# A decoder step on one core: direct fp32 head sums, another start order, and later places for solver and group-norm results

## The chip, the cores and the metric

One core of one Trainium2 chip. The metric is device time in microseconds of one execution. Five engines work side by side, each with its own instruction stream: PE (TensorE, matmuls), DVE (VectorE), ACT (ScalarE), POOL (GpSimd), SP (SyncE, here only for issuing DMAs). ACT issues DMAs too, from its own queue.

## What is computed

One layer of a hybrid decoder: an RMSNorm, one input projection, an RWKV-7 branch with 8 heads of 64, a causal pooling branch, gates, an output projection and a final norm; 2048 prompt rows and 8 x 4 sample rows, all fp32. The part around the change is the RWKV recurrence, which the kernel computes in chunks of 64 steps:

```python
h = _rmsnorm(x, norm_w)
proj = jnp.einsum('btd,de->bte', h, w_in)
...
kk = heads(k * k_k)
kk = kk * lax.rsqrt(jnp.sum(kk * kk, axis=-1, keepdims=True) + L2_EPS)
...
def _wkv_step(S, inp):
    r, w, k, v, kk, a = inp
    sa = jnp.einsum('bhvk,bhk->bhv', S, -kk)
    S = S * w[:, :, None, :] + sa[..., None] * (kk * a)[:, :, None, :] + v[..., None] * k[:, :, None, :]
    y = jnp.einsum('bhvk,bhk->bhv', S, r)
    return S, y
...
mu = jnp.mean(y, axis=-1, keepdims=True)
var = jnp.mean(jnp.square(y - mu), axis=-1, keepdims=True)
y = ((y - mu) * lax.rsqrt(var + GN_EPS)).reshape(B, T, D_RWKV) * gn_w + gn_b
bonus = jnp.sum(r * k * r_k, axis=-1, keepdims=True) * v
o_rwkv = (y + bonus.reshape(B, T, D_RWKV)) * jax.nn.silu(g_rwkv)
```

Two sums over the 64 channels of a head occur per unit of work: the sum of kk squared, called `sq`, and the bonus sum, called `bo`.

## The kernel before

The 2048 prompt rows are worked in 4 groups g of 512, the channels of the RWKV branch in 4 pairs of heads j; a **unit** (g, j) is one pair in one group, 16 in all. The projection has 25 column tiles of 128. Tile 12 (the low-rank inputs, `pp_first` in group 0) comes first in a group; then each unit projects six tiles: r, k, pooling input, v and two gates. A tile is 8 steps over the contraction, each of three matmuls of 128x128 on 128x512 in F32R: the weight is split into a rounded high part `wh` and a remainder `wl`, the input into `xh` and `xl`, and the products wh·xh, wh·xl and wl·xh are added up (L345 to L347). In group 0 the weights are loaded raw (`wr`) and split by ACT and DVE (`w_split`), and the parts are stored to memory; later groups load the stored parts.

Everything else is threaded between these matmuls. `proj` yields after each of its eight steps; this is a **slot**, and a unit has 48 of them. In each slot `side()` (L449) takes one step of every lane: the solver (`solve`), the late generators (`late`), the products (`prod`), the fold and the chain. A generator places its work by the number of its bare `yield`s; these numbers (DH, DZ, DP, YQ and constants in the code) are the table that sets the order. In a lane only the first generator runs, the others wait behind it, so a later step in one unit's solver makes those behind it later too. Each engine runs its stream in order, and an instruction whose input is not there holds up all behind it.

A unit runs as follows. `shift` takes the k tile out of PSUM into `kps` (ACT L370, DVE L371 and L373). ACT squares it into `kk2` (L533). DVE makes `abd` (L536), `cs` (L540) and both halves of `bk` (L541, L545). `key_norms` computes the head sums: `head_sums` splits its input into `hi` (ACT L472, named h_sq, h_bo) and `lo` (DVE L474, l_sq, l_bo), and `head_sums_mm` multiplies both by a block matrix of ones `bonr` (L479, L480). `products` multiplies bk by abd into `pa` (PE L588), after three yields. `solve` writes the small triangular systems to memory, reads them back as L (L647 scales them), and POOL eliminates in 31 steps into X (L654, L656); POOL then masks F and rb (L666, L668), and after YQ = 16 slots PE transposes X (`xt`, L676). Fold and `pair_chain` (L774 `ch`, `z`, `f`) carry the state through the chunks; `pair_back` normalises each head's output Y on DVE (`group_norm`, with `rsqrt_newton`'s small steps at L55 to L57, last L801) and after five yields transposes it on PE (`try`, L811). An output projection follows at the end (L1160 to L1163).

At the start `first_x` loads the eight input tiles of group 0, makes their high and low parts and their squares, and POOL adds the squares up (`acc`, L263); `first_norm` turns the sum into row sums (`xsum`, L271) and the norm's factor, by which the finished tiles are scaled. The wait of a tile for its buffer follows from the tags: `bones` shares the tag `xn` with two of the first inputs, h_sq and h_bo share `kps` with k, and l_sq and l_bo share `rps` with r.

## Time and profile before

| What | Value |
|---|---|
| Median of 3 runs | 1274.54 us (1274.52 to 1277.41) |
| The profiled execution | 1273.72 us, its span 1272.0 us |
| Mean granted TensorE clock in it | 0.972 of full speed |
| PE busy | 1186.1 us, 93% |
| DVE busy | 830.7 us, 65% |
| ACT busy | 563.4 us, 44% |
| POOL busy | 500.9 us, 39% |
| Data moved | 200.18 MB, mean 157 GB/s |

The profiled execution is one run on the chip, recorded by the hardware profiler; its span is 1.7 us shorter than its time. The page gives each engine's busy time. The list of waits gives, for an engine, what ended each stretch of idle time: the instruction that waited, what released it, the total, the number of times and the longest. A timeline row has the start, the duration, the engine, the line, the output and the inputs, and in brackets the idle time ahead of it. Durations of PE rows overlap, since matmuls are pipelined: the time that one costs is the distance between starts. The table of windows gives busy times and the granted clock of a stretch, where 1.00 is 2.4 GHz and 0.50 is 1.2 GHz.

### The profile page before, as it was taken

What the parts mean: (1) busy time and instruction counts of PE and PEld (TensorE: products, weight loads), DVE (VectorE), ACT (ScalarE), POOL (GpSimd) and SP (SyncE); (2) the same over time, 40 slices, a digit from 0 to 9 for tenths busy, and PEclk for the clock granted to TensorE, in tenths of its full rate; (3) what the DMA queues carried; (4) which work ended last, traced back from release to release, by engine and by line L of the source; (5) the groups of instructions that cost most, each with busy time, mean ns of one, the idle gap of its engine ahead of it and who ended that gap; (6) DMA issues with size and microseconds to landing.
All of it is one profiled execution on the core that took longest, in us unless ns stands there. A gap on an engine that the chain in (4) does not pass through costs nothing. (4 is left out here: it accounts for less than half of the span.)

```text
span 1272.0 us, 21094 instructions
## 1 busy us (share of the span) xinstructions
PE 1186.1 (93%) x7229; PEld 977.9 (77%) x7229; DVE 830.7 (65%) x2028; ACT 563.4 (44%) x1363; POOL 500.9 (39%) x1138
## 2 busy tenths in 40 slices
PE   7996999889989999999899899989999999999997
PEld 4765777677878788788687789889889877887685
DVE  6845767857566756866576767564656577745764
ACT  4563645444445444546353546453535453321112
POOL 6054728172343754818064708270808370000000
PEclk7997999999999999999999999999999999999999
DMA  7774555454566554546374556444444444433431
GB/s 248 236 245 138 204 184 192 155 187 153 142 208 173 169 144 144 175 150 205 116 201 140 148 154 184 131 149 126 137 130 140 121 147 151 149 112 99 131 110 66
DMA packets 153372, 200.18 MB, mean 157 GB/s; under 512 B 82480, under 2 KB 99120, under 8 KB 153264
## 3 DMA queue, kind: packets, MB, share of 16 engines
q1 hardware_dynamic: 109632, 104.90, 26.9%
q10 hardware_dynamic: 43632, 93.93, 23.6%
q8 instruction: 57, 0.93, 0.3%
q14 instruction: 51, 0.42, 0.1%
HBM read 139.39 MB, written 46.80 MB: 146 GB/s over the span
## 5 line engine op out<-in xcount | busy, mean ns | idle before, releaser
L345 PE MATMUL pp<-xh,wh 128*128 128x512 f32 (+1 forms) x992 | 366.3, 370 | 8.8 <-ACT xh L204 5.3
L346 PE MATMUL pp<-xl,wh 128*128 128x512 f32 (+1 forms) x992 | 363.4, 366 | 1.3 <-DVE xl L205 1.2
L347 PE MATMUL pp<-xh,wl 128*128 128x512 f32 (+1 forms) x992 | 362.4, 366 | 0.5 <-DVE wl L325 0.5
L345 PEld LDWEIGHTS pp<-xh,wh 128*128 128x128 f32 x992 | 189.4, 191 | 34.5 <-ACT xh L204 6.3
L346 PEld LDWEIGHTS pp<-xl,wh 128*128 128x128 f32 x992 | 189.5, 191 | 24.9 <-DVE xl L205 2.4
L347 PEld LDWEIGHTS pp<-xh,wl 128*128 128x128 f32 x992 | 189.1, 191 | 24.1 <-DVE wl L325 1.8
L654 POOL TENSOR_TENSOR Xt<-X,L 128x60 f32<-128x60 f32 (+24 forms) x496 | 186.3, 376 | 38.9
L656 POOL TENSOR_TENSOR X<-X,Xt 128x60 f32<-128x60 f32 (+24 forms) x496 | 183.0, 369 | 38.9
L649 POOL TENSOR_TENSOR X<-dmask,a 128x256 f32<-128x256 bf16 x16 | 10.8, 675 | 288.8 <-DVE a L646 288.8
L647 POOL TENSOR_TENSOR L<-L,a 128x1024 f32<-128x1024 f32 x16 | 31.8, 1990 | 170.4 <-DMA L<-dA 170.4
L774 PEld LDWEIGHTS ch<-SV,F 128*128 128x128 f32 x512 | 74.5, 191 | 18.6 <-ACT Y L778 8.5
L774 PE MATMUL ch<-SV,F 128*128 128x64 f32 x512 | 79.5, 266 | 2.2 <-DVE F L744 0.9
L741 PE MATMUL f<-zbd,ka 128*128 128x256 f32 x256 | 68.2, 387 | 0.6 <-DVE zbd L736 0.3
L1160 PE MATMUL po_o<-woh,oh_o 128*128 128x512 f32 x160 | 66.8, 418 | 0.0
L776 DVE TENSOR_TENSOR SV<-ch,lc 64x128 f32<-64x128 f32 x112 | 33.0, 295 | 51.2 <-PE ch L774 46.6
L1163 PE MATMUL po_o<-woh,ol_o 128*128 128x512 f32 x160 | 65.1, 407 | 0.2 <-DVE ol_o L1151 0.2
L1161 PE MATMUL po_o<-wol,oh_o 128*128 128x512 f32 x160 | 65.1, 407 | 0.0
L588 PE MATMUL pa<-bk,abd 128*128 128x192 f32 x256 | 54.4, 358 | 10.2 <-DVE bk L545 6.3
L736 DVE COPY zbd<-z 64x256 f32<-64x256 f32 x64 | 27.1, 427 | 53.8 <-ACT zbd L735 52.7
L778 ACT ACTIVATE Y<-ch 64x128 f32<-64x128 f32 x128 | 34.2, 267 | 61.6 <-DVE SV L776 55.7
L744 DVE TENSOR_TENSOR F<-f,F 128x512 f32<-128x512 f32 x64 | 44.2, 690 | 25.8 <-PE f L741 22.4
L588 PEld LDWEIGHTS pa<-bk,abd 128*128 128x128 f32 x256 | 47.8, 211 | 15.4 <-issue 6.6
(447 smaller groups left out, 2330.1 us busy)
## 6 DMA issues: line engine op xcount, KB each, us to landing
wh<-wh ACTq DMA_DIRECT2D x75, 512.0 KB
wl<-wl ACTq DMA_DIRECT2D x75, 512.0 KB
wr<-in_w_in ACTq DMA_DIRECT2D x25, 512.0 KB
wh<-wh SPq DMA_DIRECT2D x25, 512.0 KB
wl<-wl SPq DMA_DIRECT2D x25, 512.0 KB
xr<-in_xT SPq DMA_DIRECT2D x32, 256.0 KB
L<-dA SPq DMA_DIRECT2D x64, 128.0 KB
oi<-o_d SPq DMA_DIRECT2D x16, 512.0 KB
```

What stands on the lines that cost most here:

```text
L345: PE.matmul(pp[:, :w], hi[:, kc, :], xh[:, c], start=(kc == 0), stop=False)
L346: PE.matmul(pp[:, :w], hi[:, kc, :], xl[:, c], start=False, stop=False)
L347: mark[0] = PE.matmul(pp[:, :w], lo[:, kc, :], xh[:, c], start=False, stop=(kc == KC - 1)).ins
L588: PE.matmul(pa[:, c, :], abd[:, 2 * b + c, :], bk[:, 2 * b + c, :], start=True, stop=True)
L654: GP.tensor_tensor(out=tm, in0=X[:, :n, i:i + 1].broadcast_to([P, n, w]), in1=L[:, i + 1:, i].unsqueeze(1).broadcast_to([P, n, w]), op=mult)
L656: done = GP.tensor_tensor(out=X[:, :n, i + 1:], in0=X[:, :n, i + 1:], in1=tm, op=add).ins
L741: PE.matmul(f[:, c].rearrange("p h t -> p (h t)"), u["ka"][:, 2 * b + c, :], zbd[b % 2][:, c].rearrange("p h t -> p (h t)"), start=True, s ...
L744: V.tensor_tensor(out=d, in0=f, in1=d, op=add)
L774: PE.matmul(ch[:, h, :], fm[cc // 4][:, cc % 4, h, :], sv[cc // 4][:, cc % 4, h, :], start=True, stop=True)
L1160: PE.matmul(pp[:m], hi[:, c, :m], wh, start=(c == 0), stop=False)
L1161: mark[0] = PE.matmul(pp[:m], hi[:, c, :m], wl, start=False, stop=(both and c == 7)).ins
L1163: mark[0] = PE.matmul(pp[:n], lo[:, c, :n], wh, start=False, stop=(c == 7)).ins
```

## The change

It has four parts.

- **Head sums.** `head_sums` multiplies the fp32 input by the block matrix in one fp32 matmul; the split on ACT, the remainder on DVE and the second matmul go. `sq` is placed 4 yields after its input, `bo` 4 after that (DH 6 to 4, and without the two extra). `prod` moves to the tag `rps`.
- **Start.** A small Tanh (`warm_act`) stands first on ACT, so the activation table is loaded there. `bones` moves from tag `xn` to `cs`. The first weight tile is loaded in four parts of 128x256 and split in four parts, each ahead of the two input tiles that it meets; all eight input loads are issued ahead of the second weight; weights 1 and 2 are loaded from SP's queue. All `xh` are made by ACT; the squares come later, from the sixth input tile on. `xsum` is placed one yield later, the broadcast of the factor one less behind it.
- **Solver.** In unit (0,0) alone xt comes 12 slots later (YQ + 12).
- **Places.** `products` waits five yields in place of three, `pair_back` nine in place of five.

```diff
@@ -82,11 +82,13 @@
         for _ in range(13):
             PE.matmul(wb, wu[:, 0:P], wu, start=True, stop=True)
 
+        A.activation(sb.tile([P, 4], F32, tag="rs", name="warm_act"), wu[:, 0:4], AF.Tanh)
+
     ident = cp.tile([P, P], F32, tag="ident", name="ident")
     make_identity(nc, ident)
     ones = cp.tile([P, P], F32, tag="ones", name="ones")
     GP.memset(ones, 1.0)
-    bones = sb.tile([P, P], F32, tag="xn", name="bones")
+    bones = sb.tile([P, P], F32, tag="cs", name="bones", bufs=1)
     GP.memset(bones, 0.0)
     for h in range(2):
         GP.memset(bones[64 * h:64 * h + 64, 64 * h:64 * h + 64], 1.0)
@@ -243,34 +245,40 @@
             raw.append(sb.tile([P, 512], F32, tag=("xr", "xn", "F", "sg")[kc % 4], name=f"xr_0_{kc}",
                                bufs=3 if kc % 4 == 2 else 2))
             nc.sync.dma_start(raw[kc], xT[kc, :, 0:G])
-            if kc == 5:
-                w_load(1)
+        w_load(1)
+
+        def square(kc):
+            if kc == 0:
+                A.activation(acc, raw[kc], AF.Square)
+            else:
+                sq = sb.tile([P, 512], F32, tag="tmp", name=f"xq_{kc}", bufs=3)
+                A.activation(sq, raw[kc], AF.Square)
+                GP.tensor_tensor(out=acc, in0=acc, in1=sq, op=add)
+
         for kc, xr in enumerate(raw):
+            if kc % 2 == 0:
+                w_split_first(kc)
             w = pr[:, NW + kc:NW + kc + 1]
             hi = sb.tile([P, G], F32R, tag="xh", name=f"xh_0_{kc}", bufs=XB)
             lo = sb.tile([P, G], F32R, tag="xl", name=f"xl_0_{kc}", bufs=XB)
-            if kc >= 3:
-                V.tensor_scalar(out=hi, in0=xr, scalar1=w, scalar2=None, op0=mult)
-            else:
-                A.activation(hi, xr, AF.Identity, scale=w)
+            A.activation(hi, xr, AF.Identity, scale=w)
             V.scalar_tensor_tensor(out=lo, in0=xr, scalar=w, in1=hi.bitcast(F32), op0=mult, op1=sub)
             xs.append((hi, lo))
-            if kc == 0:
-                A.activation(acc, xr, AF.Square)
-            else:
-                sq = sb.tile([P, 512], F32, tag="tmp", name=f"xq_{kc}", bufs=3)
-                A.activation(sq, xr, AF.Square)
-                GP.tensor_tensor(out=acc, in0=acc, in1=sq, op=add)
+            if kc >= 5:
+                square(kc - 5)
+        w_split(1)
+        for kc in range(KC - 5, KC):
+            square(kc)
         return acc
 
     def first_norm(acc, segs, lst):
-        for _ in range(4):
+        for _ in range(5):
             yield
         s = bank("mm", "xsum", 2)
         for i in range(4):
             PE.matmul(s[:, i:i + 1], acc[:, i * P:(i + 1) * P], ones[:, 0:1], start=True, stop=True)
         rs = rstd_of(s, P, 4, "g0")
-        for _ in range(3):
+        for _ in range(2):
             yield
         rb0.append(bcast_rows(rs, 4, P, "g0"))
         pp = segs[0][0]
@@ -311,7 +319,21 @@
                 nc.scalar.dma_start(t.bitcast(F32), d.bitcast(F32))
         elif i < len(order):
             raws[i] = sb.tile([P, KC, P], F32, tag="wr", name=f"wr_{i}")
-            nc.scalar.dma_start(raws[i], w_in[order[i][1]])
+            if i == 0:
+                for c in range(0, KC, 2):
+                    nc.scalar.dma_start(raws[i][:, c:c + 2], w_in[order[i][1]][:, c:c + 2])
+            else:
+
+                (nc.sync if i < 3 else nc.scalar).dma_start(raws[i], w_in[order[i][1]])
+
+    def w_split_first(c):
+
+        if c == 0:
+            wts[0] = [sb.tile([P, KC, P], F32R, tag=f"w{p}", name=f"w{p}_0") for p in "hl"]
+            stores.append((wts[0], kept[order[0][1]]))
+        hi, lo = (t[:, c:c + 2] for t in wts[0])
+        A.activation(hi, raws[0][:, c:c + 2], AF.Copy)
+        V.tensor_tensor(out=lo, in0=raws[0][:, c:c + 2], in1=hi.bitcast(F32), op=sub)
 
     def w_split(i):
 
@@ -346,7 +368,8 @@
                 PE.matmul(pp[:, :w], hi[:, kc, :], xl[:, c], start=False, stop=False)
                 mark[0] = PE.matmul(pp[:, :w], lo[:, kc, :], xh[:, c], start=False, stop=(kc == KC - 1)).ins
                 if s == 0 and kc == 2:
-                    w_split(i + 1)
+                    if i:
+                        w_split(i + 1)
                     if late_load:
                         w_load(i + 2)
                 if not last or kc % 2:
@@ -406,7 +429,7 @@
             V.scalar_tensor_tensor(out=sg[:, a:a + n], in0=t1[:, a:a + n], scalar=1.0, in1=pp[:, :n], op0=add, op1=mult)
         return sg
 
-    DH, DZ, DP, YQ = 6, 2, 4, 16
+    DH, DZ, DP, YQ = 4, 2, 4, 16
 
     def c3(ap):
         return ap.rearrange("p (c t) -> p c t", t=CH)
@@ -468,16 +491,8 @@
 
     def head_sums(x, nm):
 
-        hi = sb.tile([P, 512], F32R, tag="kps", name=f"h_{nm}", bufs=1)
-        A.activation(hi, x, AF.Copy)
-        lo = sb.tile([P, 512], F32R, tag="rps", name=f"l_{nm}", bufs=1)
-        V.tensor_tensor(out=lo, in0=x, in1=hi.bitcast(F32), op=sub)
-        return hi, lo
-
-    def head_sums_mm(hl, nm):
         s = bank("mm", nm, 2)
-        PE.matmul(s, bonr, hl[0], start=True, stop=False)
-        PE.matmul(s, bonr, hl[1], start=False, stop=True)
+        PE.matmul(s, bones, x, start=True, stop=True)
         return s
 
     def decay(g, j, lst, u):
@@ -502,20 +517,18 @@
     def key_norms(g, j, u, kk2, prod):
 
         nm = f"{g}_{j}"
-        a = head_sums(kk2, f"sq_{nm}")
-        for _ in range(DH + 2):
-            yield
-        sq = head_sums_mm(a, f"sq_{nm}")
+        for _ in range(DH):
+            yield
+        sq = head_sums(kk2, f"sq_{nm}")
         sqs = sb.tile([P, 512], F32, tag="tmp", name=f"sqs_{nm}", bufs=3)
         A.activation(sqs, sq, AF.Copy)
         for h in range(2):
             for b in range(2):
                 nc.scalar.dma_start(u["dS"][b, h:h + 1],
                                     sqs[64 * h:64 * h + 1].rearrange("p (c b t) -> p b c t", b=2, t=32)[:, b])
-        a = head_sums(prod, f"bo_{nm}")
         for _ in range(DH):
             yield
-        bo = head_sums_mm(a, f"bo_{nm}")
+        bo = head_sums(prod, f"bo_{nm}")
         u["bv"] = sb.tile([P, 512], F32, tag="bv", name=f"bv_{nm}")
         A.activation(u["bv"], bo, AF.Copy)
 
@@ -546,7 +559,7 @@
         for h in range(2):
             q = slice(64 * h, 64 * h + 64)
             nc.sync.dma_start(rbd[q, :, h], rd[q])
-        prod = sb.tile([P, 512], F32, tag="pd", name=f"prod_{nm}", bufs=1)
+        prod = sb.tile([P, 512], F32, tag="rps", name=f"prod_{nm}", bufs=1)
         V.scalar_tensor_tensor(out=c3(prod), in0=rd, scalar=pr[:, RK + j:RK + j + 1],
                                in1=bk[:, :, CH:2 * CH], op0=mult, op1=mult)
         dS = dr.tile([2, 2, NCH, 32], F32, tag="dS", name=f"dS_{nm}")
@@ -575,7 +588,7 @@
     def products(g, j, u):
 
         nm = f"{g}_{j}"
-        for _ in range(3):
+        for _ in range(5):
             yield
 
         ka = sb.tile([P, NCH, P], F32, tag="ka", name=f"ka_{nm}")
@@ -667,7 +680,8 @@
             t = u["rb"][:, :, 0:CH]
             GP.tensor_tensor(out=t, in0=t, in1=mkr.unsqueeze(1).broadcast_to([P, NCH, CH]), op=mult)
 
-        for _ in range(YQ):
+
+        for _ in range(YQ if g or j else YQ + 12):
             yield
 
         for i in range(2):
@@ -804,7 +818,7 @@
         nm = f"{g}_{j}"
         yn = Y.rearrange("p a h v -> p (a h) v")
         group_norm(yn, yn, P, 8, nm)
-        for _ in range(5):
+        for _ in range(9):
             yield
         tr = bank("pt", f"try_{nm}", 2)
         for i in range(4):
@@ -1177,7 +1191,6 @@
     def main():
         st, xs = {}, []
         w_load(0)
-        w_split(0)
         acc = first_x(xs)
         low.extend(low_rank())
         for g in range(NG):
```

PE at the first solver result, unit (0,1), before. The names: pp_0_18 is the pooling tile of group 0, pair 1, and X_0_0 the solver's result of unit (0,0).

```order
L345 MATMUL pp_0_18_0_1057<-xh_0_6_281,wh_9_1008 128x512
L346 MATMUL pp_0_18_0_1057<-xl_0_6_282,wh_9_1008 128x512
L347 MATMUL pp_0_18_0_1057<-xh_0_6_281,wl_9_1009 128x512
L676 MATMUL xt_0_0_0_1102<-ident_84,X_0_0_686 32x128 x4
L676 MATMUL xt_0_0_1_1111<-ident_84,X_0_0_686 32x128 x4
L345 MATMUL pp_0_18_0_1057<-xh_0_7_288,wh_9_1008 128x512
L346 MATMUL pp_0_18_0_1057<-xl_0_7_289,wh_9_1008 128x512
L347 MATMUL pp_0_18_0_1057<-xh_0_7_288,wl_9_1009 128x512
```

And now, where pp_0_22 is the fifth tile of the same unit (ident is a unit matrix):

```order
L368 MATMUL pp_0_22_0_1190<-xl_0_4_267,wh_11_1146 128x512
L369 MATMUL pp_0_22_0_1190<-xh_0_4_266,wl_11_1147 128x512
L690 MATMUL xt_0_0_0_1212<-ident_86,X_0_0_704 32x128 x4
L367 MATMUL pp_0_22_0_1190<-xh_0_5_270,wh_11_1146 128x512
L368 MATMUL pp_0_22_0_1190<-xl_0_5_271,wh_11_1146 128x512
L369 MATMUL pp_0_22_0_1190<-xh_0_5_270,wl_11_1147 128x512
L367 MATMUL pp_0_22_0_1190<-xh_0_6_277,wh_11_1146 128x512
L368 MATMUL pp_0_22_0_1190<-xl_0_6_278,wh_11_1146 128x512
L369 MATMUL pp_0_22_0_1190<-xh_0_6_277,wl_11_1147 128x512
L367 MATMUL pp_0_22_0_1190<-xh_0_7_284,wh_11_1146 128x512
L368 MATMUL pp_0_22_0_1190<-xl_0_7_285,wh_11_1146 128x512
L690 MATMUL xt_0_0_1_1221<-ident_86,X_0_0_704 32x128 x4
```

The two transposes have moved from the end of the unit's third tile into its fifth, 47 projection matmuls on, and five matmul steps apart from each other; sq, bo and pa of unit (0,1) and the broadcast of the next group's factor now stand ahead of them.

PE at the start of unit (0,2) before, where pp_0_10 is its fourth tile; bk and abd are the inputs of pa.

```order
L345 MATMUL pp_0_10_0_1822<-xh_0_0_241,wh_16_1751 128x512
L346 MATMUL pp_0_10_0_1822<-xl_0_0_242,wh_16_1751 128x512
L479 MATMUL sq_0_2_1792<-h_sq_0_2_1733,bonr_95 128x512
L347 MATMUL pp_0_10_0_1822<-xh_0_0_241,wl_16_1752 128x512
L345 MATMUL pp_0_10_0_1822<-xh_0_1_246,wh_16_1751 128x512
L588 MATMUL pa_0_2_0_1760<-bk_118,abd_108 128x192 x2
L588 MATMUL pa_0_2_1_1768<-bk_118,abd_108 128x192 x2
L480 MATMUL sq_0_2_1792<-l_sq_0_2_1735,bonr_95 128x512
```

And now, first at sq and then at bo and pa (two stretches of the stream):

```order
L367 MATMUL pp_0_19_0_1689<-xh_0_7_284,wh_15_1589 128x512
L495 MATMUL sq_0_2_1723<-kk2_0_2_1670,bonr_97 128x512
L368 MATMUL pp_0_19_0_1689<-xl_0_7_285,wh_15_1589 128x512
L369 MATMUL pp_0_19_0_1689<-xh_0_7_284,wl_15_1590 128x512
L367 MATMUL pp_0_10_0_1803<-xh_0_0_246,wh_16_1710 128x512
```

```order
L367 MATMUL pp_0_10_0_1803<-xh_0_3_260,wh_16_1710 128x512
L495 MATMUL bo_0_2_1777<-prod_0_2_1684,bonr_97 128x512
L368 MATMUL pp_0_10_0_1803<-xl_0_3_261,wh_16_1710 128x512
L369 MATMUL pp_0_10_0_1803<-xh_0_3_260,wl_16_1711 128x512
L367 MATMUL pp_0_10_0_1803<-xh_0_4_266,wh_16_1710 128x512
L368 MATMUL pp_0_10_0_1803<-xl_0_4_267,wh_16_1710 128x512
L369 MATMUL pp_0_10_0_1803<-xh_0_4_266,wl_16_1711 128x512
L825 MATMUL try_0_0_1740<-ident_86,Y_0_0_1308 128x128 x4
L601 MATMUL pa_0_2_0_1758<-bk_120,abd_110 128x192 x2
L367 MATMUL pp_0_10_0_1803<-xh_0_5_270,wh_16_1710 128x512
L368 MATMUL pp_0_10_0_1803<-xl_0_5_271,wh_16_1710 128x512
L601 MATMUL pa_0_2_1_1766<-bk_120,abd_110 128x192 x2
```

sq takes kk2 itself and stands in the third tile, bo also stands earlier (before, it came 54 rows behind the first half of sq), and pa stands further back, behind try of unit (0,0), which before was read 48 rows ahead of sq, in the k tile.

DVE between k's shift and bk in the same unit before; nwt and st are group_norm's small tiles of 128x8, and th1 is the low-rank factor.

```order
L371 SCALAR_TENSOR_TENSOR kps_0_6_1711<-pp_0_6_0_1675,pr_144,t1_0_6_1710 128x511
L373 SCALAR_TENSOR_TENSOR kps_0_6_1711<-carry_156,pr_144,t1_0_6_1710 128x1
L375 COPY carry_156<-pp_0_6_0_1675 128x1
L536 SCALAR_TENSOR_TENSOR abd_108<-kps_0_6_1711,pr_144,lam_162 64x8x64 x2
L540 TENSOR_TENSOR cs_0_2_1596<-kps_0_6_1711,cs_0_2_1596 128x512
L541 TENSOR_TENSOR bk_118<-cs_0_2_1596,ab_0_2_1720 128x8x64
L545 TENSOR_TENSOR bk_118<-cs_0_2_1596,th1_0_2_1623 128x8x64
L474 TENSOR_TENSOR l_sq_0_2_1735<-kk2_0_2_1716,h_sq_0_2_1733 128x512
L550 SCALAR_TENSOR_TENSOR prod_0_2_1730<-rd_0_2_1724,pr_144,bk_118 128x512
```

And now:

```order
L396 SCALAR_TENSOR_TENSOR kps_0_6_1665<-carry_158,pr_146,t1_0_6_1664 128x1
L55 TENSOR_TENSOR nwt_0_0_1622<-st_0_0_1614 128x8
L398 COPY carry_158<-pp_0_6_0_1564 128x1
L549 SCALAR_TENSOR_TENSOR abd_110<-kps_0_6_1665,pr_146,lam_164 64x8x64
L56 SCALAR_TENSOR_TENSOR nwt_0_0_1622<-nwt_0_0_1622,st_0_0_1614 128x8
L549 SCALAR_TENSOR_TENSOR abd_110<-kps_0_6_1665,pr_146,lam_164 64x8x64
L57 SCALAR_TENSOR_TENSOR st_0_0_1614<-nwt_0_0_1622,st_0_0_1614 128x8
L553 TENSOR_TENSOR cs_0_2_1442<-kps_0_6_1665,cs_0_2_1442 128x512
L55 TENSOR_TENSOR nwt_0_0_1622<-st_0_0_1614 128x8
L554 TENSOR_TENSOR bk_120<-cs_0_2_1442,ab_0_2_1674 128x8x64
L56 SCALAR_TENSOR_TENSOR nwt_0_0_1622<-nwt_0_0_1622,st_0_0_1614 128x8
L558 TENSOR_TENSOR bk_120<-cs_0_2_1442,th1_0_2_1476 128x8x64
```

Between kps and bk five of group_norm's small steps of unit (0,0) now alternate with the unit's own; the remainder l_sq is gone.

## Rows read from the trace of the kernel before

**Rows 1.** The page's first part: busy us, share of the span, instructions.

```profile
PE 1186.1 (93%) x7229; PEld 977.9 (77%) x7229; DVE 830.7 (65%) x2028; ACT 563.4 (44%) x1363; POOL 500.9 (39%) x1138
```

**Rows 2.** PE's waits: for what; us in total, times, longest us.

```profile
PE try L811 <- DVE Y L801: 13.3, 13, 2.1
PE xt L676 <- POOL X L656: 11.8, 1, 11.8
PE sq L479 <- ACT h_sq L472: 7.9, 3, 3.3
PE pa L588 <- DVE bk L545: 6.3, 2, 3.2
...
PE pp_first L345 <- ACT wh L324: 4.3, 1, 4.3
PE try L811 <- DVE carry L375: 4.2, 1, 4.2
```

**Rows 3.** Stages: start:end, length, busy (count) by engine, granted clock, DMA share, GB/s.

```profile
0.00:30.00 30.00, 20.51 (x51) 11.13 (x52) 21.27 (x30) 12.52 (x20) 19.77 (x53) 0.77 0.76 263
...
112.00:300.00 188.00, 172.14 (x992) 137.16 (x991) 137.30 (x296) 89.14 (x196) 90.76 (x201) 0.96 0.53 173
...
600.00:900.00 300.00, 283.56 (x1976) 248.12 (x1974) 193.14 (x471) 138.38 (x368) 134.34 (x302) 0.98 0.52 152
...
106.00:112.00 6.00, 5.58 (x19) 4.31 (x20) 2.37 (x7) 3.67 (x10) 3.97 (x5) 0.58 0.01 3
```

**Rows 4.** PE timeline at the first sq: start us, duration us, line, output<-inputs.

```profile
56.62 0.40 PE L347 MATMUL pp<-xh,wl 128*128 128x512 f32 x1
56.85 0.46 PE L479 MATMUL sq<-h_sq,bonr 128*128 128x512 f32 x1
57.15 0.39 PE L345 MATMUL pp<-xh,wh 128*128 128x512 f32 x1
```

**Rows 5.** PE timeline at a pooling matmul (L862, fp32).

```profile
68.81 1.02 PE L862 MATMUL po<-d,pw 128*128 128x512 f32 x2
69.67 0.38 PE L619 MATMUL pb<-rbd,bk 128*128 128x128 f32 x2
```

**Rows 6.** Timelines of ACT, POOL and PE in the first 31 us.

```profile
7.53 1.28 ACT L255 ACT_TABLE_LOAD   x1 [7.53 <-DMA xr<-in_xT]
8.83 0.72 ACT L255 ACTIVATE xh<-xr,pr 128x512 fp32r<-128x512 f32 x1
...
17.51 9.37 POOL L263 TENSOR_TENSOR acc<-acc,xq 128x512 f32<-128x512 f32 x6
...
10.55 0.79 PE L345 MATMUL pp_first<-xh,wh 128*128 128x512 f32 x1 [4.35 <-ACT wh L324]
...
30.42 0.28 PE L271 MATMUL xsum<-ones,acc 128*128 128x1 f32 x2
```

**Rows 7.** PE timeline around the first solver result.

```profile
94.26 0.40 PE L347 MATMUL pp<-xh,wl 128*128 128x512 f32 x1
106.42 1.89 PE L676 MATMUL xt<-ident,X 128*32 128x128 f32 x8 [11.76 <-POOL X L656]
```

**Rows 8.** The page's part 5: POOL's first step on L, sixteen units.

```profile
L647 POOL TENSOR_TENSOR L<-L,a 128x1024 f32<-128x1024 f32 x16 | 31.8, 1990 | 170.4 <-DMA L<-dA 170.4
```

**Rows 9.** Timelines of POOL and DVE at two unit starts and one group_norm.

```profile
601.51 2.54 POOL L666 TENSOR_TENSOR F<-F,mkr 64x512 f32<-64x512 f32 x2
...
601.67 2.40 DVE L57 SCALAR_TENSOR_TENSOR rs_g<-nwt_g,rs_g 128x4 f32<-128x4 f32 x1
...
608.43 0.68 DVE L545 TENSOR_TENSOR bk<-cs,th 128x512 f32<-128x512 f32 x1
...
422.76 0.75 DVE L371 SCALAR_TENSOR_TENSOR kps<-pp,pr,t 128x511 f32<-128x511 f32 x1 [0.93 <-ACT t L370]
...
426.74 0.78 DVE L545 TENSOR_TENSOR bk<-cs,th 128x512 f32<-128x512 f32 x1
...
218.63 0.17 DVE L56 SCALAR_TENSOR_TENSOR nwt<-nwt,st 128x8 f32<-128x8 f32 x1
```

## The prediction

> **What bounds the kernel now.** The page's busy shares come first: PE 93%, DVE 65% [rows 1]. PE is the bound, so 85.9 of 1272.0 us (1272.0 − 1186.1) are PE idle, and a change can win that idle time, the time lost to the low clock, and nothing else unless it takes work off PE. The second view is PE's list of waits [rows 2]: it says which idle time ends with what. Nearly all of the large entries belong to four places. try waits for the normalised Y (13.3 us in 13 short pieces) and once for carry (4.2 us); xt waits once, 11.8 us, for X from the POOL solver; the unit starts wait for h_sq (7.9 us, 3 times) and for bk (6.3 us, twice), and the first tile waits 4.35 us for its weight [rows 6]. The third view is the table by stages [rows 3], with the granted clock beside the busy time. 0 to 30 us runs at 0.77 of full speed, 106 to 112 at 0.58, 112 to 300 at 0.96, 600 to 900 at 0.98. A wait is therefore paid twice: after an idle stretch the clock stands at its lower level (1.2 GHz) for a while. In 106 to 112 that costs (1 − 0.58) x 6 = 2.5 us on top of the wait.
>
> **Head sums.** Before, each of 32 sums is an ACT split, a DVE remainder and two F32R matmuls; now one fp32 matmul. What PE pays before: matmul starts lie 0.23 us apart in plain projection work (56.62 to 56.85), and the first half of a sum, among matmuls of other forms, takes 0.30 (56.85 to 57.15) [rows 4], so 0.46 to 0.60 us a sum. What it pays after: the pooling matmul (L862) is an fp32 matmul of the same 128x512 form, shown as two records, and the next one starts 0.86 us later (68.81 to 69.67) [rows 5]. The difference is 0.26 to 0.40 us. The fp32 sum will stand among other forms too, so its 0.86 may carry friction as well; I take 0.34 us, the middle: 32 x 0.34 = **+11** (8.3 to 12.8). It lies wholly on PE, which is the bound, so nothing hides it. The Trainium skill ("FP8 and Floating Point Precision", section "TensorE Precision Notes") says that true FP32 takes four passes through the array. Four passes at the 0.23 us above would be 0.92, and by it the term would be an estimated 32 x 0.46 = 14.7 at most and the time 1254; the row with 0.86 is a little lower. The ACT and DVE work that is removed (32 splits and 32 remainders of one 128x512 pass each) lies on engines with room; its worth is that sq no longer waits for h_sq.
>
> **Start.** Before, the activation table is loaded at 7.53, after the first x tile landed, for 1.28 us; the first projection matmul starts at 10.55; the POOL sum of squares runs its last six adds from 17.51 for 9.37 us, to 26.88; PE reaches xsum at 30.42 [rows 6]. 39 projection matmuls stand ahead of xsum, 39 x 0.23 = 9.0 us at full clock, done in 19.9. An xh pass on ACT is 0.72 us. Now the table is loaded without data, the first weight comes and is split in quarters, all eight x loads go out ahead of wr_1, and ACT makes all xh, which frees DVE for xl. PE then follows DVE and ACT (eight passes of 0.72 and four quarters of the weight, about 7.5 us of work, from about 7.5 on) and has its first tile by about 16.5; 18 matmuls of the next tile stand ahead of xsum, so PE would be there at about 21. But the adds on POOL start only after the squares, which now come after the sixth xh: about 13 + 7 x 9.37/6 = 24. So POOL's adds, not PE, set xsum at 24 or 25 in place of 30.42 (and three matmuls more are done by then): **−6.5** (−4 if DMA serves the quarters late, −9 if the adds run at their shortest). The loads of wr_1 and wr_2 move to SP's queue, wr_1 right behind the x loads, wr_2 behind lw, lwx, pw and the two stores of the first tile, which wait for the last quarter of wl. The first tile's 24 matmuls and the wait for POOL's adds cover both, so I cost this at nothing, and at up to +2 if the stores hold wr_2 back (the range has it).
>
> **First solver result.** xt_0_0 stands after 12 more slots; by the order, between old and new place lie 47 projection matmuls, the sq, bo and pa of unit (0,1) and the row broadcast, about 47 x 0.23 + 2 x 0.86 + 3 = 15 us of PE work. The wait is 11.76 us, behind a last matmul that starts at 94.26 [rows 7]. If X ends as much earlier as the start gains, the wait is gone with its clock fall: −11.8 − 2.5 = −14. Against it: sq_0_1 now stands ahead of xt and needs kk2_0_1 from ACT, which in its own queue waits for an xt_g load behind stores, up to 3 us. Taken **−12** (−6 to −14). The solver lane keeps its lag, so later results of the solver are read later too; [rows 2] show one wait for X in the whole program, so that wins nothing more, and the chain behind it only moves.
>
> **Unit starts.** sq no longer needs h_sq: its input kk2 is ready before bk. The 7.9 us go. pa stands two slots later, so part of the 6.3 us goes. What is next late: bk. On DVE the chain from kps to bk takes 422.76 to 427.52 = 4.8 us undisturbed, and from the stretched op at 601.67 to 609.11 = 7.4 us where a small DVE op (L57) lasts 2.40 beside a POOL mask of 2.54 [rows 9]. By the order the masks now fall behind the unit start, since the solver lane lags by 12 slots more. Against the gain: group_norm's small ops now stand between kps and bk in 11 of 16 units (the order pieces on DVE show one), 3 to 6 of them at some 0.2 us (0.17 in [rows 9]), so bk comes 0.6 to 1.2 us later. By the order PE has 5.7 to 9 us of work between the end of k and the first pa in most units, and in the last six 5.7 to 6.4, against some 1 us for the shift's first pass + 4.8 + 0.9 = 6.7 us to bk: six waits of half a us or so come new. 7.9 + 6.3 = 14.2 and about 2 of clock go; six new waits cost 3, and of the two long bk waits I leave about 4 standing: **−9** (0 to −16). Units where POOL stretches a DVE op as at 601.67 may still come: **+1** (0 to +8).
>
> **try four slots later.** The order gives PE about 1 us more of work between the last ch and try in the mean (2 us in half of the units, none in a few). The waits are 13.3 in 13, 1.0 each, 2.1 the longest: that covers about two thirds, and the carry wait of 4.2 (a DVE op stretched beside POOL) goes if the mask no longer falls there. group_norm now shares DVE with the kps chain, which takes some back. 0.6 x 17.5 = 10.5: **−9** (−2 to −16).
>
> **Sum** on the profiled execution (1273.7, span 1272.0; the median of the runs is 0.8 above it): +11 − 6.5 − 12 − 9 + 1 − 9 = −24.5, so 1249.2 profiled and **1250** as median. Half of every term's way to its ends, added, gives about ±13 for this case: 1237 to 1263.
>
> **Rivals.**
> - *The waits come back as waits for DVE* (chance 0.12). Every unit start ends at bk, and try at a group_norm that shares DVE; then the unit starts win nothing and try only 3: +11 − 6.5 − 11 + 0 − 3 + 3 = −6.5, 1268. For it: DVE's unit start is the next thing that is late by less than 1 us. Against: DVE has 35% of its time free and loses the 32 remainders.
> - *The solver's end doesn't move* (0.14). POOL's first step on L waits for the load of L in every unit (170.4 us in all, [rows 8]); if that load, not PE, sets the end of X, it stays at 106.4 while PE comes about 7 us earlier. PE arrives at 94.7 − 7 + 15 = 103, and waits 3.7 us, with the clock fall 6.2 in place of 14.3: X term −8 in place of −12, 1254.
> - *Slower* (0.10). bk late by more than PE's filler in every unit: the fp32 sums are paid in full (+12.8), the start and X win 6.5 + 11 = 17.5, try and sq nothing. With d us more of pa wait per unit the time is slower by over 3.8 us from 16 x d > 17.5 − 12.8 + 3.8 on, that is d above 0.53. At d = 1 us it would be +11.3, 1286. What decides is whether pa waits for bk in all 16 units. For it: 11 units have group_norm rows inside the chain. Against: in ten units PE's filler ahead of pa is longer than the chain by one to four us.
> - *More* (0.14). With few waits left the clock stays up everywhere: start −9, X −14, unit starts −14, try −15, sums +9 = −43, 1232.
>
> **How the numbers follow.** My forecast has 0.50, the rivals 0.14, 0.14, 0.12, 0.10. Within 0.3% (3.8 us, about what a measurement of this kernel can tell from no change) lies about half of the first rival and a little of the last: same 0.07; slower 0.10; faster 0.83. The range holds the forecast, the unmoved solver and about half of the DVE rival, and about half of "more": 1231 to 1268; outside stay half of "more" (0.07) and the slower one (0.10).
>
> **What the profile after would show.** Right: first projection matmul by 8 to 9, xsum at 24 or 25, released by POOL acc; no wait for X over 3 us; no wait of sq over 1 us; pa waits for bk short and spread over several units; try waits under 7 us in all; PE busy time up by 6 to 13 us less what the clock gives back; two fp32 records per sum with the next matmul 0.86 us on. Wrong: a wait of xt near 5 us (solver unmoved), a list of waits led by pa for bk with over 12 us (DVE rival), or a clock under 0.97 with few waits.

## The result: 0.9% to 1.3% faster, half of what was forecast, and the profile after

The changed kernel takes 1264.33 us in the median (1261.16 to 1266.79, 4 runs) against 1275.97 for the kernel before (1274.52 to 1281.42, 4 runs). The ratio is 0.9891 with a 95% interval of 0.9869 to 0.9913: 11.6 us less, where 24.5 were forecast. Sign and range (1231 to 1268) held, the size did not.

The profiled execution took 1265.87 us, a little above its median, and the one of before 1273.72, a little below; their spans differ by 7.9 us. The busy times on the page of the changed kernel, as [rows 1]:

```profile
PE 1201.0 (95%) x7229; PEld 974.4 (77%) x7229; DVE 783.2 (62%) x1994; ACT 548.7 (43%) x1340; POOL 478.0 (38%) x1138
```

PE's idle time is 1264.1 − 1201.0 = 63.1 us, 22.8 less than before. But PE's busy time is 14.9 more. The table of windows in steps of 5 us splits that: the sum of busy time times granted clock, the work at full speed, goes from 1160.9 to 1173.0 (+12.1, the fp32 sums), and the busy time lost to the low clock from 25.1 to 28.1 (+3.0). −22.8 + 12.1 + 3.0 = −7.7, the difference of the spans but for rounding. PE's waits, as [rows 2]:

```profile
PE sq L495 <- ACT kk L546: 9.4, 8, 2.4
PE pp L369 <- DVE wl L347: 4.7, 4, 1.8
PE try L825 <- DVE Y L815: 4.6, 3, 1.9
PE ch L788 <- ACT Y L792: 4.4, 10, 2.6
PE pp L367 <- DVE carry L398: 3.2, 1, 3.2
PE q L709 <- DVE X L703: 3.2, 4, 2.0
PE pa L601 <- DVE st L808: 3.0, 2, 2.6
```

The wait for X and the carry wait of try are gone, and the wait for Y has fallen from 13.3 to 4.6. The wait of sq is not gone: it now ends with kk2 (which the row calls kk), 9.4 us in 8 pieces where it was 7.9 in 3. New or longer are waits for wl, of `ch`, for carry at a projection tile, and of the solver's step q. All rows of the two lists, added up by the instruction that waited (they hold 76.0 and 53.5 us, all but some 10 us of the idle time in each):

| PE waits (us) | before | after | difference |
|---|---|---|---|
| projection tiles (pp, pp_first) | 18.5 | 10.3 | −8.2 |
| xt | 11.8 | 0 | −11.8 |
| sq, bo and pa (unit starts) | 19.0 | 21.3 | +2.3 |
| try | 17.5 | 4.6 | −12.9 |
| ch and q (chain, solver) | 3.7 | 10.0 | +6.3 |
| all others | 5.5 | 7.3 | +1.8 |

And the stages, as [rows 3]:

```profile
0.00:30.00 30.00, 23.11 (x70) 13.94 (x71) 17.22 (x36) 17.65 (x31) 20.81 (x53) 0.87 0.77 259
...
112.00:300.00 188.00, 176.53 (x1019) 136.86 (x1018) 134.72 (x293) 92.89 (x206) 90.99 (x203) 0.99 0.57 179
...
600.00:900.00 300.00, 289.48 (x1983) 249.65 (x1982) 171.27 (x448) 133.32 (x361) 128.94 (x332) 0.97 0.50 147
```

The first 30 us run at 0.87 in place of 0.77 and 112 to 300 at 0.99 in place of 0.96, but 600 to 900 at 0.97 in place of 0.98: between these two executions the clock's loss has moved, not fallen.

### The profile page after: what moved, and what is told of

The parts are those of the page before. It is cut to its first block, busy times and chain, and to the rows that moved or that the text cites. A ratio compares the mean times of both kernels' runs of the same rounds, so it can differ in the third digit from the quotient of the medians.

```text
span 1264.1 us, 20999 instructions
## 1 busy us (share of the span) xinstructions
PE 1201.0 (95%) x7229; PEld 974.4 (77%) x7229; DVE 783.2 (62%) x1994; ACT 548.7 (43%) x1340; POOL 478.0 (38%) x1138
## 4 chain that ended last, share of the span: by engine, by line
PE 66%; DVE 14%; ACT 7%; DMA 6%; issue 2%; POOL 2%; ACTq 1%; SPq 1%; DVEq 0%; POOLq 0%
PE pp L369 10%; PE pp L367 10%; PE pp L368 10%; PE po_o L1174 5%; PE po_o L1175 4%; PE po_o L1177 4%; PE f L755 4%; PE ch L788 3%; PE pa L601 3%; PE z L747 2%; DMA xr<-in_xT 2%; ACT rb L636 2%; DVE abd L549 1%; DMA L<-dA 1%; ACT F L634 1%
## 5 line engine op out<-in xcount | busy, mean ns | idle before, releaser
L367 PE MATMUL pp<-xh,wh 128*128 128x512 f32 (+1 forms) x992 | 378.8, 383 | 3.2 <-DVE carry L398 3.2
L369 PE MATMUL pp<-xh,wl 128*128 128x512 f32 (+1 forms) x992 | 369.9, 373 | 4.7 <-DVE wl L347 4.7
L368 PE MATMUL pp<-xl,wh 128*128 128x512 f32 (+1 forms) x992 | 371.2, 374 | 0.6 <-DVE xl L207 0.4
L367 PEld LDWEIGHTS pp<-xh,wh 128*128 128x128 f32 x992 | 191.2, 193 | 32.4 <-issue 9.9
L667 POOL TENSOR_TENSOR Xt<-X,L 128x60 f32<-128x60 f32 (+24 forms) x496 | 176.6, 356 | 38.9
L669 POOL TENSOR_TENSOR X<-X,Xt 128x60 f32<-128x60 f32 (+24 forms) x496 | 169.4, 341 | 38.9
L602 ACT ACTIVATE Ab<-pa 128x128 f32<-128x128 f32 x64 | 17.1, 277 | 93.5 <-PE pa L601 56.9
L601 PEld LDWEIGHTS pa<-bk,abd 128*128 128x128 f32 x256 | 42.4, 191 | 18.5 <-issue 10.8
```

Of the source, the lines that this page charges most:

```text
L367: PE.matmul(pp[:, :w], hi[:, kc, :], xh[:, c], start=(kc == 0), stop=False)
L368: PE.matmul(pp[:, :w], hi[:, kc, :], xl[:, c], start=False, stop=False)
L369: mark[0] = PE.matmul(pp[:, :w], lo[:, kc, :], xh[:, c], start=False, stop=(kc == KC - 1)).ins
L601: PE.matmul(pa[:, c, :], abd[:, 2 * b + c, :], bk[:, 2 * b + c, :], start=True, stop=True)
L667: GP.tensor_tensor(out=tm, in0=X[:, :n, i:i + 1].broadcast_to([P, n, w]), in1=L[:, i + 1:, i].unsqueeze(1).broadcast_to([P, n, w]), op=mult)
L669: done = GP.tensor_tensor(out=X[:, :n, i + 1:], in0=X[:, :n, i + 1:], in1=tm, op=add).ins
```

## The experiments

Eleven other kernels and the changed kernel once more, each timed beside the kernel before on its own chip. The record has three: chip 11 for the four only_ kernels, chip 0 for undo_yq, undo_back, no_sums and sq_later, chip 12 for after_again, undo_prod, sums_early and split_early. The kernel before had medians of 1278.7, 1278.2 and 1278.4 us there (1270 to 1287 in all), so ratios to it are compared across the three. The last three columns are of the profiled execution of each; "work" is busy time times clock as above, "lost" the busy time less that. One execution stands for each kernel there: that of sq_later lies 9.9 us and that of only_back 8.2 us above its kernel's median, the others within 4.4 us of theirs.

| Kernel | ratio to before | 95% interval | PE idle | work | lost |
|---|---|---|---|---|---|
| before | 1 | | 85.9 | 1160.9 | 25.1 |
| changed, first comparison | 0.9891 | 0.9869 to 0.9913 | 63.1 | 1173.0 | 28.1 |
| after_again | 0.9915 | 0.9882 to 0.9948 | 63.4 | 1173.6 | 25.7 |
| only_start | 0.9936 | 0.9912 to 0.9960 | 84.6 | 1162.2 | 20.2 |
| only_yq | 1.0029 | 1.0001 to 1.0057 | 89.9 | 1164.4 | 23.9 |
| only_back | 0.9998 | 0.9969 to 1.0026 | 94.4 | 1160.7 | 30.7 |
| only_sums | 1.0059 | 1.0025 to 1.0092 | 87.7 | 1171.3 | 22.2 |
| sums_early | 0.9924 | 0.9894 to 0.9953 | 77.0 | 1168.9 | 23.2 |
| undo_yq | 0.9914 | 0.9885 to 0.9944 | 69.3 | 1169.1 | 30.4 |
| undo_back | 0.9955 | 0.9926 to 0.9985 | 67.6 | 1173.0 | 31.7 |
| undo_prod | 0.9923 | 0.9889 to 0.9957 | 69.7 | 1172.6 | 26.5 |
| no_sums | 0.9979 | 0.9944 to 1.0014 | 85.4 | 1162.0 | 32.4 |
| split_early | 0.9988 | 0.9959 to 1.0018 | 80.5 | 1164.1 | 27.0 |
| sq_later | 1.0018 | 0.9984 to 1.0051 | 80.6 | 1173.3 | 34.5 |

### The parts, each alone on the kernel before

**only_start**: the start part of the diff and nothing else.

```diff
+A.activation(sb.tile([P, 4], F32, tag="rs", name="warm_act"), wu[:, 0:4], AF.Tanh)
-bones = sb.tile([P, P], F32, tag="xn", name="bones")
+bones = sb.tile([P, P], F32, tag="cs", name="bones", bufs=1)
...
+                w_split_first(kc)
...
-            if kc >= 3:
-                V.tensor_scalar(out=hi, in0=xr, scalar1=w, scalar2=None, op0=mult)
```

> The kernel before with the start part alone (early table load, first weight in quarters, all x loads first, xh on ACT, squares later). Theory 'the start is won for good': xsum released by POOL acc at 25 to 26 us in place of 30.4, and 5 to 7 us less in all (ratio 0.995), the X wait stays near 11.8. Rival 'the solver's end does not move': POOL's X still ends near 106, the wait of xt for X grows to 16 or more, and the time stays within 2 us of before.

Measured 0.9936, some 8 us less, a little more than the 5 to 7 expected. PE's waits:

```profile
PE xt L699 <- POOL X L679: 11.6, 2, 11.2
PE pa L611 <- DVE bk L568: 9.1, 3, 3.4
```

The start is won alone and the wait for X stays, as the first theory had it: X ends 3 us earlier (xt starts at 103.45, before at 106.42 [rows 7]), and PE is there 2.4 us earlier; pa's wait for bk has even grown from 6.3 [rows 2] to 9.1.

**only_yq**: the 12 slots and nothing else.

```diff
-        for _ in range(YQ):
+        for _ in range(YQ if g or j else YQ + 12):
             yield
```

> The kernel before with xt of unit (0,0) 12 slots later and nothing else. Theory 'the X wait is simply gone': no wait of xt for X above 1 us, PE idle less by 10 to 12 us, time less by 10 to 13 us (ratio 0.991). Rival 'put off, not won': the work put off comes back in the later units, the other waits of PE grow by half of it, and the time is less by 3 to 6 us only.

Measured 1.0029: neither theory; it is no faster, and its interval (from 1.0001) barely tells it from no change. The wait for X is gone, and PE's idle time is 4.0 us larger.

```profile
PE try L812 <- DVE Y L802: 18.5, 9, 4.1
PE try L812 <- DVE pcarry L842: 7.4, 2, 3.8
PE sq L479 <- ACT h_sq L472: 7.1, 4, 5.4
```

try waits 18.5 + 7.4 = 25.9 us where it waited 17.5. By the order all later chains are put off with the solver's lane, so that their group_norm meets the unit starts; that this is the reason was not tried. sq of unit (0,1), next in line at 99 us, waits 5.4 of the 11.8 us at once. A wait of 11.8 us, taken away, is worth nothing by itself here.

**only_back**: nine yields in pair_back.

```diff
         group_norm(yn, yn, P, 8, nm)
-        for _ in range(5):
+        for _ in range(9):
             yield
```

> The kernel before with pair_back's nine yields in place of five. Theory: the try waits (17.5 us in 14) fall below 6 and the time by 8 to 11 us. Rival: group_norm's steps and try now fall into the unit starts, waits of sq, pa and other tiles take over, and the time is within 4 us of before.

Measured 0.9998, the rival. try's waits fall only from 17.5 to 14.0 in all, and projection tiles wait 23.8 where they waited 18.5.

**only_sums** and **sums_early**: the direct sums at the places of before, and at their new ones. Beyond the diff of `head_sums`, in key_norms of the first:

```diff
-        a = head_sums(kk2, f"sq_{nm}")
         for _ in range(DH + 2):
             yield
-        sq = head_sums_mm(a, f"sq_{nm}")
+        sq = head_sums(kk2, f"sq_{nm}")
```

and in the second also:

```diff
-    DH, DZ, DP, YQ = 6, 2, 4, 16
+    DH, DZ, DP, YQ = 4, 2, 4, 16
...
-        for _ in range(DH + 2):
+        for _ in range(DH):
```

> The kernel before with the direct fp32 head sums, at the places that they had (nine slots for sq, six more for bo). Theory 'the wait was for the split': the sq waits (7.9 us) go, PE work grows by 32 x 0.27 = 8.6 us, and the time is within 3 us of before. Rival 'the wait was for the place': sq still waits for kk2 or pa takes over the wait for bk (6.3 us today, then 12 or more), and the time is 6 to 10 us longer.

Measured 1.0059, the rival's range. Work grew by 1171.3 − 1160.9 = 10.4 us, and pa took over the wait:

```profile
PE try L801 <- DVE Y L791: 18.9, 14, 4.3
PE xt L666 <- POOL X L646: 15.5, 1, 15.5
PE pa L578 <- DVE bk L535: 11.1, 5, 3.3
...
PE sq L472 <- ACT kk L523: 3.3, 2, 1.8
```

> The kernel before with the direct head sums at their new, early places (sq four slots after its input, bo four more) and nothing else of the change. With the sums at the old places it was 1.006. Theory 'the early place is what wins, not the form': sq then fills PE while DVE makes bk, pa waits under 6 us (11.1 with the old places), ratio 0.992 to 0.999. Rival 'the unit start only works with pa and try moved too': pa still waits 9 us or more, ratio 1.002 to 1.010.

Measured 0.9924, at the good end of the first theory's range. The same arithmetic with sq four slots earlier and bo six is 1.3% faster, the intervals far apart:

```profile
PE try L801 <- DVE Y L791: 13.5, 14, 4.4
PE xt L666 <- POOL X L646: 12.4, 1, 12.4
PE sq L472 <- ACT kk L523: 6.1, 4, 2.5
PE pa L578 <- DVE bk L535: 6.0, 3, 3.2
```

sq waits longer (6.1 for 3.3) and pa half as long for bk (6.0 for 11.1), try waits 13.5 for 18.9, xt 12.4 for 15.5. In PE's rows sq starts ahead of the first pa in all sixteen units, in only_sums in twelve; that PE then has the sum to do while bk is made fits these waits. The form is the same in both and the work differs little (1168.9 and 1171.3), so with the direct form the place wins it. What the place is worth without that form, split_early asks below.

### One part taken out of the changed kernel

**after_again**: the changed kernel itself, unedited, on chip 12.

> The changed kernel itself once more, beside the kernels of this call and of the last two on the same chip, so that they are compared with it there and not across chips. Expected 0.989 of before as in the first comparison (0.987 to 0.991); if it is 0.995 or more here, the gains seen so far hold for one chip or one hour only.

Measured 0.9915, just past the expected range and short of 0.995; the result holds here too.

**undo_yq**: YQ for all units.

```diff
-        for _ in range(YQ if g or j else YQ + 12):
+        for _ in range(YQ):
```

> The changed kernel with the 12 slots taken out again (xt of unit (0,0) at its old place). The changed kernel stands at 0.989 of before. Theory 'the parts need each other' (the later xt pays only with try further back): xt waits 10 to 12 us for X, the try waits grow again, ratio 0.996 to 1.000. Rival 'the 12 slots are worth nothing here either, as alone': the X wait is back but what it costs is won later, ratio 0.987 to 0.992.

Measured 0.9914, the rival. The wait for X returns, but at 5.7 us:

```profile
PE try L824 <- DVE Y L814: 9.7, 7, 4.0
PE xt L689 <- POOL X L669: 5.7, 1, 5.7
```

With the sums early, sq, bo and the first half of pa of unit (0,1) stand ahead of xt even without the 12 slots (PE starts them at 93.42, 99.67 and 97.63, xt at 106.41), and cover half. The 12 slots are worth nothing that these intervals show.

**undo_back**: five yields in pair_back.

```diff
-        for _ in range(9):
+        for _ in range(5):
```

> The changed kernel with pair_back at five yields again. Theory 'the parts need each other': the try waits go from 4.6 us to 18 or more, as in the kernel with the later xt alone (25.9), ratio 0.998 to 1.003. Rival 'the places of group_norm are worth nothing, as alone': try waits some 8 us more, others less, ratio 0.988 to 0.992.

Measured 0.9955, between the two ranges, and slower than the changed kernel's first interval; the interval of after_again overlaps it. try is back as the first theory said:

```profile
PE try L825 <- DVE Y L815: 20.4, 11, 4.2
```

So the nine yields take 15.8 us of try's waits away where the later xt stands too (4.6 against 20.4), though alone they take 3.5. That the time follows is likely and not clear of the intervals.

**undo_prod**: three yields ahead of pa.

```diff
         nm = f"{g}_{j}"
-        for _ in range(5):
+        for _ in range(3):
             yield
```

> The changed kernel with three yields ahead of the products (pa) in place of five. Theory 'what stands ahead of pa covers DVE's unit start': pa's waits for bk and group_norm (9.5 us over all) grow to 15 or more, ratio 0.993 to 0.998. Rival 'pa's place does not matter': 0.987 to 0.991.

Measured 0.9923, between the two and not to be told from the changed kernel; pa's waits add up to 12.3, for 9.5 in the changed kernel and 7.2 in its second profile.

**no_sums**: the head sums and their places as before, all else as changed.

```diff
-    DH, DZ, DP, YQ = 4, 2, 4, 16
+    DH, DZ, DP, YQ = 6, 2, 4, 16
...
+        hi = sb.tile([P, 512], F32R, tag="kps", name=f"h_{nm}", bufs=1)
+        A.activation(hi, x, AF.Copy)
+        lo = sb.tile([P, 512], F32R, tag="rps", name=f"l_{nm}", bufs=1)
+        V.tensor_tensor(out=lo, in0=x, in1=hi.bitcast(F32), op=sub)
```

> The changed kernel with the head sums as they were (split on ACT and DVE, two F32R matmuls, sq nine slots after its input, bo six more), all else as changed. Theory 'the fp32 sums cost and win nothing': PE busy falls by 8 us or so, the sq waits for h_sq stay under 9.4 us, ratio 0.982 to 0.986. Rival 'they take ACT and DVE work off the unit starts, which PE waits for': pa and sq wait 8 us and more beyond the changed kernel, ratio 0.988 to 0.995.

Measured 0.9979, past the rival's range. The work falls by 11.0 to 1162.0 and the idle time grows by 22.3:

```profile
PE try L835 <- DVE Y L825: 15.3, 8, 4.4
PE sq L502 <- ACT h_sq L495: 8.8, 4, 4.5
```

The waits of try add up to 18.2 (4.6 in the changed kernel), of pa to 12.9 (9.5); sq's hardly change.

**split_early**: split sums, but at the new places.

```diff
-        for _ in range(DH + 2):
+        for _ in range(DH):
             yield
         sq = head_sums_mm(a, f"sq_{nm}")
```

(the split's lines otherwise as in no_sums, DH = 4)

> The changed kernel with the sums split again (ACT, DVE, two F32R matmuls) but left at the new, early places. Theory 'the direct form is needed for the early place': sq waits for h_sq in most units, 15 us or more in all, ratio 0.994 to 1.000. Rival 'the place alone wins': PE busy 7 us lower than in the changed kernel, sq's waits below 12, ratio 0.982 to 0.988, faster than both kernels.

Measured 0.9988, the first theory's range, though not by its mechanism: sq's waits are 7.6 in all and not 15.

```profile
PE pa L611 <- DVE bk L568: 5.8, 4, 3.6
...
PE bo L503 <- DVE l_bo L497: 4.9, 3, 3.1
PE sq L502 <- ACT h_sq L495: 4.8, 5, 1.5
```

pa waits 14.7 in all, bo 4.9, try 8.0. In the changed kernel the early place without the direct form is worth nothing that shows (0.9988, and 0.9979 with neither, in no_sums); the direct form at a later place, next, is worth as little.

**sq_later**: sq three slots later, bo two.

```diff
-        for _ in range(DH):
+        for _ in range(DH + 3):
             yield
         sq = head_sums(kk2, f"sq_{nm}")
...
-        for _ in range(DH):
+        for _ in range(DH - 1):
             yield
         bo = head_sums(prod, f"bo_{nm}")
```

> The changed kernel with sq three slots later (seven yields in place of four, and bo two slots later than now). Theory 'sq stands too early': its waits for kk2 (9.4 us in 8) fall below 3, pa's and bo's do not grow by as much, ratio 0.983 to 0.986. Rival 'the unit start is DVE's': the wait for kk2 comes back at pa for bk or group_norm's steps, ratio 0.988 to 0.991.

Measured 1.0018, slower than either theory allowed, the whole gain of the change gone.

```profile
PE pa L601 <- DVE ka L603: 5.9, 4, 3.0
...
PE pa L601 <- DVE bk L558: 4.5, 2, 3.1
PE sq L495 <- ACT kk L546: 4.0, 5, 2.1
```

sq's waits do fall, to 4.0, but pa's add up to 19.3 (9.5 in the changed kernel). The loss to the clock, 34.5 us for 28.1, is that of the slowest of its ten executions: the mean granted clock of all ten is 0.973, the profiled one's 0.967. In PE's rows sq still starts ahead of the first pa in fourteen of the sixteen units; in the last two pa comes first and waits 1.84 and 1.89 us. So the order of the two explains the smaller part of pa's longer waits, and the rest stays open, as does the share of bo, which moved too.

## Why the prediction was right in sign and wrong in size, step by step

**What bounds: right.** PE stays the bound at 95%, and what is won between the two profiled executions is idle time (22.8 us); the fp32 sums give half of it back (12.1).

**Head sums: right in price, wrong in worth.** The place at 597 us, PE's timeline:

```profile
597.57 1.02 PE L495 MATMUL sq<-kk,bonr 128*128 128x512 f32 x2
598.03 0.79 PE L369 MATMUL pp<-xh,wl 128*128 128x512 f32 x1
598.66 0.39 PE L367 MATMUL pp<-xh,wh 128*128 128x512 f32 x1
```

The sum and the next matmul take 1.09 us (597.57 to 598.66) and the sum so 0.86, as [rows 5] had it; it shows partly as the length of the row behind it. The work grew by 12.1 us, and 8.0 and 10.4 in the two kernels with the sums alone, against 11 (8.3 to 12.8) forecast; kernels with the same matmuls differ by up to 4.5 us in it (1169.1 in undo_yq, 1173.6 in after_again). But the prediction said that their worth was that sq no longer waits for h_sq. sq waits as long as before (9.4 us, 8.8 before). The sums pay only as direct form and early place together. On the kernel before, the form alone is at 1.0059 and both at 0.9924. With the other parts changed, neither is at 0.9979 (no_sums), the place alone at 0.9988 (split_early), the form at later places at 1.0018 (sq_later), and both at 0.9915. In try's waits, 18.2 us in no_sums and 4.6 in the changed kernel, 10.2 of the 13.6 us go with the place already (8.0 in split_early) and 3.4 with the 32 splits and 32 remainders. Why the time needs both stays open: between split_early and the changed kernel PE's idle time falls by 17.4 us in small pieces, 5.2 of them at pa.

**Start: right.** Forecast −6.5, alone 0.9936 or 8 us. xsum is released by POOL's adds at 25.56, forecast 24 or 25, and PE has its first matmul at 6.45, two us earlier than forecast. Two PE rows:

```profile
6.45 0.49 PE L367 MATMUL pp_first<-xh,wh 128*128 128x512 f32 x1 [0.22 <-ACT xh L264]
...
25.56 0.38 PE L279 MATMUL xsum<-ones,acc 128*128 128x1 f32 x2 [1.70 <-POOL acc L256]
```

**The first solver result: the wait went, the reason given did not hold.** The condition was that X ends as much earlier as the start gains. POOL's first steps of unit (0,0) before, and then after with its last and PE's xt:

```profile
71.50 0.67 POOL L649 TENSOR_TENSOR X<-dmask,a 128x256 f32<-128x256 bf16 x1 [44.62 <-DVE a L646]
75.97 2.09 POOL L647 TENSOR_TENSOR L<-L,a 128x1024 f32<-128x1024 f32 x1 [3.80 <-DMA L<-dA]
```

```profile
63.30 0.68 POOL L662 TENSOR_TENSOR X<-dmask,a 128x256 f32<-128x256 bf16 x1 [37.80 <-DVE a L659]
75.32 2.79 POOL L660 TENSOR_TENSOR L<-L,a 128x1024 f32<-128x1024 f32 x1 [11.34 <-DMA L<-dA]
...
109.62 0.24 POOL L669 TENSOR_TENSOR X<-X,Xt 128x8 f32<-128x8 f32 x1
...
110.06 0.60 PE L690 MATMUL xt<-ident,X 128*32 128x128 f32 x4
```

In the changed kernel POOL is ready 8.2 us earlier (63.30 for 71.50) and then waits 11.34 us for the load of L, to 75.32 in place of 75.97. So the elimination starts when that load has landed, as the rival "the solver's end does not move" had it. X does not end earlier even so, but later: at 109.86 (109.62 + 0.24) for 106.4 before, since POOL's 64 instructions from L on take 34.5 us for 30.4; in that stretch DVE is busy 26.1 us for 14.0. The work put ahead of xt just covered this, which was luck: xt starts at 110.06, 0.2 us behind the end of X (2.6 us in the second profile). What the wait was worth was mis-sized: only_yq and undo_yq give nothing for it, and in only_yq the sq and try behind it wait in its place. Its −12 was one wait of one execution, read as if what comes next were not late.

**Unit starts: the step that failed.** Forecast −9 with +1 for disturbed units, measured +2.3 in the waits of sq, bo and pa: 10.3 of the some 17 us that are missing between the two profiled executions (−24.5 forecast, −7.9 measured). The waits of ch and q (+6.3), which the sum did not have, and the clock are most of the rest, less what try won beyond its forecast. Two sentences of the term are wrong. "The 7.9 us go": sq lost its wait for h_sq, but was itself put four slots earlier, where kk2 is the late one. "The masks now fall behind the unit start": they do so by the order of POOL's stream, but in time they fall on it. POOL, DVE and PE rows of the changed kernel at unit (0,3):

```profile
211.21 2.54 POOL L679 TENSOR_TENSOR F<-F,mkr 64x512 f32<-64x512 f32 x2
213.72 1.80 POOL L681 TENSOR_TENSOR rb<-rb,mkr 128x512 f32<-128x512 f32 x1
...
211.41 2.37 DVE L810 SCALAR_TENSOR_TENSOR st<-st 128x8 f32<-128x8 f32 x1
...
214.30 1.25 DVE L811 TENSOR_SCALAR st<-st 128x8 f32<-128x8 f32 x1
...
216.60 0.74 DVE L394 SCALAR_TENSOR_TENSOR kps<-pp,pr,t 128x511 f32<-128x511 f32 x1
...
218.27 1.12 PE L495 MATMUL sq<-kk,bonr 128*128 128x512 f32 x2 [2.37 <-ACT kk L546]
```

While POOL masks F and rb (211.21 to 215.52), two of group_norm's steps on 128x8 elements last 2.37 and 1.25 us, 0.16 or 0.17 in the median of the sixteen units; kps comes after them and a split of a weight (1.21 us) at 216.60, and sq waits 2.37 us for what is made from it. The same at unit (3,0), where a step of the shift on one column and one of group_norm are stretched, and the next tile waits 3.25 us for the carry:

```profile
783.80 2.54 POOL L679 TENSOR_TENSOR F<-F,mkr 64x512 f32<-64x512 f32 x2
...
783.88 1.32 DVE L396 SCALAR_TENSOR_TENSOR kps<-carry,pr,t 128x1 f32<-128x1 f32 x1
785.12 1.24 DVE L57 SCALAR_TENSOR_TENSOR st<-nwt,st 128x8 f32<-128x8 f32 x1
...
788.33 0.57 PE L367 MATMUL pp<-xh,wh 128*128 128x272 f32 x1 [3.25 <-DVE carry L398]
```

Four of the larger waits of the changed kernel follow such rows at once (sq 2.26, 2.37 and 1.10, a tile 3.25 us, 9.0 in all); in its second profile it is three (sq 2.38, 1.10 and 2.03, 5.5 in all). By the Trainium skill ("SBUF — State Buffer", section "Who interferes with whom") a VectorE op with two SBUF inputs contends with a GpSimd op that reads SBUF, as does one that runs in a two-port mode, which a tensor_scalar can; the one issued first then blocks the other for its whole length. The stretched rows agree, one of them a TENSOR_SCALAR with one input; the step of 2.37 us lasts nearly as long as two masks one behind the other (2.54). That the masks' place costs these 9.0 or 5.5 us is read from the trace and was not tried: no kernel here moved them. Nor is it new. Before, two waits follow such rows at once, the first behind a step of 2.42 us at 222.17, the second behind that of 2.40 at 601.67 [rows 9]:

```profile
226.54 0.63 PE L811 MATMUL try<-ident,Y 128*128 128x128 f32 x4 [4.25 <-DVE carry L375]
...
608.49 0.50 PE L479 MATMUL sq<-h_sq,bonr 128*128 128x512 f32 x1 [3.26 <-ACT h_sq L472]
```

That is 7.5 us, so by this reading the masks' cost has moved to other units, where the forecast had it all but gone.

**try: forecast −9, measured −12.9 in waits**, but only in company. Alone the nine yields win nothing, with the later xt alone try gets worse (25.9), and only both with the sums at their early places bring 4.6 (8.0 where those are split). That terms add up was itself a step of the prediction, and it failed: only_start and sums_early alone are worth 0.64% and 0.76%, the whole 0.9% to 1.1%, so that the later xt, the nine yields and the five yields together add nothing that can be seen to these two. Without the sums they even seem to cost: no_sums, which is only_start with these three, is at 0.9979. A kernel with just the start and the early sums was not run.

**The clock: open.** Up to 4.5 us of it were counted inside the terms (2.5 at xt, 2 at the unit starts). The profiles show none: 28.1 and 25.7 us of PE's busy time were lost in the two of the changed kernel, for 25.1 in the one before. Two of the new waits let it fall: the granted clock is 0.71 in 659 to 663, behind the 2.55 us of pa, and 0.50 (1.2 GHz) in 788 to 792, behind the 3.25 us of the tile; behind sq's 2.37 us it stays at 1.00 in 218 to 222. But a profile is one execution. Over all that were timed on chip 12 the mean granted clock is 0.974 in the changed kernel (6) and 0.969 in the one before (19), and 0.005 of 1264 us is some 6 us, an estimate. So the clock may well have given back what the prediction counted on.

**Which rival.** The time lies nearest to "the waits come back as waits for DVE" (1268), and its mechanism is the one that the rows show, at sq and pa; its second half, at try, did not come. The range held because it was drawn to take in half of this rival, not because the sum was right.

**What stays open.** Why the waits of ch and q grew by 6.3 us; why the sums need both form and place, and how much of sq_later's loss is bo's place; why POOL's elimination takes longer after the change; and whether the masks elsewhere, or start and early sums alone, would be faster than the changed kernel. Of those run none is clearly faster than it; undo_yq, undo_prod and sums_early are not told from it by their intervals.

## What to carry to other kernels

A list of waits prices each wait as if it stood alone. Where several engines are late by about as much, removing one wait exposes the next, and parts that win nothing alone can pay together, as the form of the sums and their place do here (and the other way round): cost a term by what is late next at that place, and test parts singly and by taking each out. An operation that has its input early can be worth more as filler ahead of a wait than its own wait costs (sq's waits grew by 2.8 us and pa's for bk fell by 5.1 from only_sums to sums_early): try it there, and look where another engine's long operations fall in time, which the order of its stream does not tell.
